# The MLP residual of a decoder trunk: added up in SBUF, or gathered per group and added in DRAM by accumulating DMAs

## The chip, the cores and the metric

One Trainium2 chip, one of its cores. The metric is the device time of one execution in microseconds (us), lower is better. Before the change three executions took 2427.35, 2429.12 and 2431.06 us; the median is 2429.12 us.

## The reference

A two-layer decoder trunk, sequence 1024, width 1024, all in float32. Layer 0 mixes with an mLSTM, layer 1 with differential attention that reads a K/V shared between layers. Both layers end in the same MLP, and that is all that the change touches:

```python
y = modulate(rms_norm(x, norm_mlp_g[layer]), sh2, sc2)
x = x + g2 * sq_relu_mlp(y, mlp_w_up[layer], mlp_w_down[layer])   # square(relu(y @ w_up)) @ w_down
```

`x` is 1024 x 1024, `w_up` 1024 x 4096, `w_down` 4096 x 1024; the gate `g2` is one number for each column of `x`. After layer 0, `x` goes on to the attention layer, after layer 1 to the final norm.

## The kernel before, in words

Everything is kept transposed: a tile has 128 of the 1024 features on its partitions and 512 tokens along its free axis. The residual `xt` (the tile `x` of the profile) is one SBUF tile of 128 x 2 halves of the tokens x 8 feature blocks (nb) x 512, 4 MB. Each matmul is done three times, as high x high, low x high and high x low part of a split of both operands (`mm3`, lines 183 to 185), so each weight that arrives as `wraw`, `e` or `m` is split by ScalarE (ACT, line 170, the high part: `wh`, `eh`, `lh`) and then VectorE (DVE, line 171, the rest: `wl`, `el`, `ll`).

The MLP's 4096 hidden features are cut into 8 groups of 4 blocks. For groups 1 to 7 of each layer a group runs as follows. **Up** (`group_up`): 8 products of 24 matmuls for 4 weight blocks f0 to f3 and two halves; ACT takes relu and square, and ACT and DVE make from the results the operands `bh`, `bl`, `th`, `tl`. **Down** (`down`): the output's 8 blocks are taken as 4 pairs, 0 to 3; each pair's product is a 2 x 2 block product of Strassen's kind in Winograd's form, with 7 products instead of 8, each of 6 matmuls (3 for each of k = 0, 1). The seven of a pair are numbered 1 to 7, and `PSEQ` lists the order (pair, product) of all 28, which interleaves the pairs. The results of products 1, 6, 7 and 4 pile up in one PSUM bank, and those of 5 and 3 in another; after each product the bank as it stands is added, times the gate, into one of the pair's four cells of `xt` (`add`, line 675): cell (half 0, first block) receives 1 and 2, (half 1, first) 6 and 3, (half 1, second) 7 and 5, (half 0, second) 4. All 28 additions are DVE instructions that read PSUM and read and write `xt`.

A pair's weights come in two loads of 256 KB, `e` and `m` (lines 652, 653). DVE builds from them four sums in chain (lines 654 to 657: `m`, `e`, `e`, `m`), ACT and DVE split both into `eh`, `el` (needed by products 1, 2, 5, 6) and `lh`, `ll` (3, 4, 7). Raw and split weights share one pool of nine 4 KB buffers (`wp`), so a load can only be issued once the tile nine allocations before it has been read for the last time. In layer 0 the same pool also carries the `adar` loads (line 149), background work of 512 KB each for the conditioning.

Group 8 goes another way: up as before, down as a plain product (`gemm`) whose consumer `residual` adds into `xt` with DVE (line 585) and starts the sum of squares for the next norm.

Nothing of the order is written out beyond this. A scheduler (`schedule_with_timeline_sim=True`) puts the instructions on the engines' queues by its own simulation, so the same source line can land in another place when something near it changes. All loads and stores before the change are issued on SP's queue, which takes them strictly in order.

Of the kernel before, what the change touches and what calls it, by code (L numbers as in the profile page):

```python
# [12 lines left out]
ALU = mybir.AluOpType  # L13
# [41 lines left out]
def tile_yoco(ctx: ExitStack, tc: tile.TileContext, x, c, pos, cst, vec, bg, lp, ada,  # L55
              w_in, w_v0, w_v, w_o, w_mo, w_kv, w_vb, w_q, w_do, w_up, w_dn, out):
    nc = tc.nc
    pe, act, dve, sp = nc.tensor, nc.scalar, nc.vector, nc.sync
# [6 lines left out]
    def gps():  # L65
        return pools["g"].tile([P, HT], F32, tag="g", name="gps")
# [28 lines left out]
    xdr = dr.tile([P, 2, NB, HT], F32, tag="xdr", name="xdr")  # L95
# [66 lines left out]
    def mcol(l, which, nb):  # L162
        return mod[:, l * 48 + which * 8 + nb:l * 48 + which * 8 + nb + 1]
# [18 lines left out]
    def mm3(ps, wh, wl, a, b, first, last, more=False):  # L182
        pe.matmul(ps, lhsT=wh, rhs=a, start=first, stop=False, skip_group_check=more)  # L183
        pe.matmul(ps, lhsT=wh, rhs=b, start=False, stop=False, skip_group_check=more)  # L184
        pe.matmul(ps, lhsT=wl, rhs=a, start=False, stop=last, skip_group_check=more)  # L185
# [132 lines left out]
    def load_x(xt, src):  # L318
        for half in range(2):
            for k in range(0, NB, 4):  # L320
                sp.dma_start(out=xt[:, half, k:k + 4], in_=src[:, half, k:k + 4])
# [8 lines left out]
    xt = xp.tile([P, 2, NB, HT], F32, tag="x", name="x")  # L330
# [93 lines left out]
    with ExitStack() as ph:  # L424
# [39 lines left out]
        with ExitStack() as ph1:  # L464
            trp = ph1.enter_context(tc.tile_pool(name="tr", bufs=1))
            rows = trp.tile([AH, 3, T], F32, tag="rows", name="rows")
            for j, src in enumerate((ic, lf)):
                for half in range(2):
                    ps = pm.tile([P, HT], F32, tag="mb", name="rps")
# [4 lines left out]
            ps = pm.tile([P, HT], F32, tag="mb", name="mps")  # L474
# [4 lines left out]
        ps = pm.tile([P, HT], F32, tag="mb", name="mps")  # L479
# [117 lines left out]
    def mlp(np_, l, xt, slot, nbg, ends, args, before=None, tail=None, closing=()):  # L597
# [3 lines left out]
        with ExitStack() as ph:  # L601
# [16 lines left out]
                dve.tensor_tensor(out=out, in0=a, in1=b, op=ALU.subtract)  # L618

            quads = {}  # L620

            def quad_out(f, half, ps):
                j, q = f // 2, quads.setdefault(f // 2, {})
                q[f % 2, half] = squared(ps)

                def keep(hs, ls, i, src):
                    split(hs[:, i, j], ls[:, i, j], src)

                if (0, 0) in q and (0, 1) in q and "t1" not in q:
                    q["t1"] = scratch("t1")  # L630
                    sub(q["t1"], q[0, 1], q[0, 0])
                    keep(th, tl, 0, q["t1"])
                if (0, 0) in q and (1, 0) in q and "v" not in q:
                    q["v"] = scratch("v")
                    sub(q["v"], q[1, 0], q[0, 0])
                    keep(bh, bl, 0, q[0, 0])
                    keep(bh, bl, 1, q[1, 0])
                if (1, 1) in q:
                    b22, t1, t3, v = q[1, 1], q["t1"], q[0, 1], q["v"]
                    sub(t1, b22, t1)  # L640
                    keep(th, tl, 1, t1)
                    sub(t3, b22, t3)
                    sub(v, v, t3)
                    keep(th, tl, 2, t3)
                    keep(bh, bl, 2, b22)
                    keep(th, tl, 3, v)
                    del quads[j]
# [20 lines left out]
                      7: (th, tl, 2)}  # L668

            def down(pairs, ready):  # L670
                banks = {}

                def add(ps, half, nb):
                    xs = xt[:, int(half), nb]
                    dve.scalar_tensor_tensor(xs, ps, mcol(l, 5, nb), xs, ALU.mult, ALU.add)  # L675

                for i, p in PSEQ:
                    if p == 1:
                        if i + 1 < 4:
                            pairs[i + 1] = pairs[i + 1]()  # L680
                        else:
                            ready()
                    c = {1: "X", 6: "X", 7: "X", 4: "X", 5: "Y", 3: "Y", 2: "Z"}[p]
                    fresh = (i, c) not in banks
                    if fresh:
                        banks[i, c] = gps()
                    ps = banks[i, c]
                    wh, wl, wi = pairs[i][p]
                    hh, hl, hi = moving[p]
                    for k in range(2):  # L690
                        mm3(ps, wh[:, k, wi], wl[:, k, wi], hh[:, hi, k], hl[:, hi, k], fresh and k == 0,
                            k == 1, not fresh)
                    add(ps, p in (6, 7, 5, 3), 2 * i + (p in (7, 4, 5)))

            def dn_src(gi, nb, pat, **kw):
                b = ((gi * NB) + nb) * P * P * FN
# [24 lines left out]
            for gi in range(FG - 1):  # L721
                srcs = [[dn_src(gi, 2 * i + j, "(p q r c) -> p q r c", q=2, r=2) for j in range(2)] for i in range(4)]
                for got in group_up(gi, w0, steady if gi else first, lambda: pair_load(srcs[0])):
                    if isinstance(got, dict):
                        pairs = [got] + [lambda i=i: pair_load(srcs[i]) for i in range(1, 4)]
                    else:
                        quad_out(*got)
                nxt = []
                down(pairs, lambda: nxt.append(wload(w_up[l, FN * (gi + 1)], [P, NB, P], nbg and nbg + 1)))
                w0 = nxt[0]  # L730

            hh = hp.tile([P, 2, FN, HT], F32R, tag="th", name="hh")
            hl = hp.tile([P, 2, FN, HT], F32R, tag="tl", name="hl")
            sums = hp.tile([P, 2, HT], F32, tag="bh", name="sums")
            acc[:] = [sums[:, 0], sums[:, 1]]
            srcs = [dn_src(FG - 1, nb, "(p k c) -> p k c", k=FN) for nb in range(NB)]
            gi = FG - 1
            for got in group_up(gi, w0, steady, lambda: None):
                if got is None:
                    continue  # L740
                f, half, ps = got
# [14 lines left out]
    def resident(ph, name):  # L756
        xp = ph.enter_context(tc.tile_pool(name="xp" + name, bufs=1))
        np_ = ph.enter_context(tc.tile_pool(name="np" + name, bufs=6))
        pools["g"] = ph.enter_context(tc.tile_pool(name="pg" + name, bufs=7, space=PSUM))
        pools["n"] = ph.enter_context(tc.tile_pool(name="pn" + name, bufs=1, space=PSUM))  # L760
        rings.append(np_)
        return xp.tile([P, 2, NB, HT], F32, tag="x", name="x"), np_
# [3 lines left out]
    xt, np_ = resident(l0, "1")  # L766
# [15 lines left out]
    def q_norm(half):  # L782
# [5 lines left out]
        return f  # L788

    mlp(np_, 0, xt, 1, 2, ((0,), (1,)), {(1,): dict(hooks={1: q_norm(0)})}, lambda: scale_cols(3, 48 + 8, V_NMIX + 8),  # L790
        q_norm(1), (accs, vps))
    assert not pend
# [88 lines left out]
    with ExitStack() as ph:  # L881
# [172 lines left out]
        for i in range(len(seq) + 2 + LAG):  # L1054
# [17 lines left out]
            while norms and norms[0][0] < i - LAG:  # L1072
                h, half = norms[0][1:3]
# [19 lines left out]
    with ExitStack() as ph:  # L1093
        xt, np_ = resident(ph, "2")
        load_x(xt, xdr)
        scale_cols(4, 48 + 32, V_NMLP + 8)
        gemm([w_do[n] for n in range(8)], NB, yhk, ylk, residual(np_, xt, lambda nb: mcol(1, 2, nb), True), 0,
             (1,), hooks={1: mlp_norm(np_, 1, xt, 4)})

        def scaled(part, rb):  # L1100
            half, c0, c1 = (part, 0, HT) if isinstance(part, int) else part
            for k in range(NB):
                xs = cut(xt, part, k)
                dve.scalar_tensor_tensor(xs, xs, vc[:, V_FIN + k:V_FIN + k + 1], rb, ALU.mult, ALU.mult)
                if k % 2:
                    sp.dma_start(out=out[:, half, k - 1:k + 1, c0:c1], in_=cut(xt, part, slice(k - 1, k + 1)))

        ends = (1, 0, CUT), (1, CUT, HT)
        rbs = []
        def finish():  # L1110
            with tc.issue_after(added[0].ins):
                rbs.append(rstd_of(np_, ends[1]))
                for part, rb in zip(ends, rbs):
                    scaled(part, rb)

        mlp(np_, 1, xt, 4, 0, ((0,), ends), {ends: dict(
            hooks={1: lambda: scaled(0, rstd_of(np_, 0))}, sizes=LSZ,
            after={(len(LSZ) - 1, ends[0]): lambda: rbs.append(rstd_of(np_, ends[0]))})}, tail=finish,
            closing=(accs,))
# [99 lines left out]
```

## Time and profile before

| what | value |
|---|---|
| three executions, median | 2429.12 us (2427.35 to 2431.06) |
| the profiled execution's own time | 2429.98 us |
| its span, first to last instruction | 2428.2 us |
| TensorE (PE) busy | 2367.1 us, 97% |
| VectorE (DVE) busy | 1559.4 us, 64% |
| ScalarE (ACT) busy | 989.2 us, 41% |
| GpSimd (POOL) busy | 0.2 us; it issues nothing |
| DMA | 266.81 MB, 110 GB/s over the span |
| the changed line's group, L675 | 392 instructions, 286.8 us, 746 ns each |

The MLP of layer 0 runs from about 480 to 1160 us of the span, that of layer 1 from about 1740 to 2428 us. Times in a timeline are microseconds from the start of the span; a row has its start, its length, the engine, the line, the operation, output<-inputs and, in brackets, how long the engine had been idle before and what released it. SPq is SP's queue of DMA issues; its length is the issue, not the transfer.

### The profile page before, as it was taken

The numbers are of one execution on the slowest core, as the hardware profiler recorded it, in microseconds if no ns is written. First come the engines' busy times: TensorE is split into PE (matmuls) and PEld (weight loads), VectorE is DVE, ScalarE is ACT, GpSimd is POOL, SyncE is SP. The second block draws the span as 40 slices with busy tenths as digits, with TensorE's granted clock in tenths as the row PEclk, the third lists the DMA queues.
The fourth block names the chain that finished last, engine by engine and source line by source line (L and its number), as shares of the span: only waits on it lengthen the run. The fifth ranks groups of instructions, "written<-read, shape, count | busy, mean of one in ns | idle before, by whom it ended". The sixth has DMA issues, their size and how long they took to land.

```text
span 2428.2 us, 30918 instructions
## 1 busy us (share of the span) xinstructions
PE 2367.1 (97%) x12018; PEld 1983.7 (82%) x12018; DVE 1559.4 (64%) x2576; ACT 989.2 (41%) x1898; POOL 0.2 (0%) x4
## 2 busy tenths in 40 slices
PE   7999999999999999999999999999999999999997
PEld 4899998788888888887788899987778888878886
DVE  7436544787877787767653367664775567566647
ACT  4325633444324323424332467763434323432423
POOL 0000000000000000000000000000000000000000
PEclk9999999999999999999999999999999999999999
DMA  7312242313322342234454654764111111111113
GB/s 306 120 64 77 79 148 78 122 51 119 135 95 79 130 139 75 90 113 143 153 178 154 176 162 148 217 196 160 65 57 35 61 61 44 39 61 57 35 53 122
DMA packets 117150, 266.81 MB, mean 110 GB/s; under 512 B 12426, under 2 KB 51850, under 8 KB 115212
## 3 DMA queue, kind: packets, MB, share of 16 engines
q1 hardware_dynamic: 117004, 264.84, 33.5%
q8 instruction: 94, 1.54, 0.3%
q14 instruction: 52, 0.43, 0.1%
HBM read 228.03 MB, written 36.77 MB: 109 GB/s over the span
## 4 chain that ended last, share of the span: by engine, by line
PE 90%; DVE 3%; DMA 3%; ACT 2%; issue 1%; SPq 1%; DVEq 0%; ACTq 0%
PE gps L183 24%; PE gps L185 24%; PE gps L184 24%; PE gps L255 3%; PE gps L256 3%; PE gps L257 3%; PE gps L971 2%; PE sc L930 1%; PE sc L931 1%; PE tps L957 1%; DMA kb<-kdr 1%; DVE adar L336 1%; PE hps L528 1%; DMA wraw<-in_w_do_dram 1%; PE hps L530 1%
## 5 line engine op out<-in xcount | busy, mean ns | idle before, releaser
L183 PE MATMUL gps<-yh,wh 128*128 128x512 f32 x1664 | 657.4, 399 | 7.9 <-ACT yh L301 5.0
L184 PE MATMUL gps<-yl,wh 128*128 128x512 f32 x1664 | 658.5, 396 | 0.7 <-DVE yl L302 0.7
L185 PE MATMUL gps<-yh,wl 128*128 128x512 f32 x1664 | 655.3, 396 | 0.7 <-DVE wl L171 0.7
L183 PEld LDWEIGHTS gps<-yh,wh 128*128 128x128 f32 x1664 | 313.6, 189 | 85.4 <-ACT yh L301 5.9
L185 PEld LDWEIGHTS gps<-yh,wl 128*128 128x128 f32 x1664 | 313.4, 188 | 78.7 <-DVE wl L171 1.1
L184 PEld LDWEIGHTS gps<-yl,wh 128*128 128x128 f32 x1664 | 313.5, 188 | 76.7 <-issue 1.2
L170 ACT CAST wh<-wraw 128x1024 fp32r<-128x1024 f32 (+2 forms) x176 | 170.6, 970 | 473.7 <-DMA wraw<-in_w_up_dram 208.9
L171 DVE TENSOR_TENSOR wl<-wraw,wh 128x1024 fp32r<-128x1024 f32 (+2 forms) x176 | 198.1, 1126 | 206.3 <-ACT wh L170 204.5
L675 DVE SCALAR_TENSOR_TENSOR x<-gps,mod,x 128x512 f32<-128x512 f32 x392 | 286.8, 746 | 59.7 <-PE gps L185 58.1
L255 PE MATMUL gps<-wh,yh 128*128 128x256 f32 (+1 forms) x768 | 224.9, 293 | 4.8 <-ACT sv L841 3.4
L256 PE MATMUL gps<-wl,yh 128*128 128x256 f32 (+1 forms) x768 | 220.6, 287 | 0.0
L257 PE MATMUL gps<-wh,yl 128*128 128x256 f32 (+1 forms) x768 | 219.9, 286 | 0.0
L170 ACT CAST eh<-e 128x1024 fp32r<-128x1024 f32 x56 | 58.8, 1049 | 240.9 <-DVE e L656 240.9
L150 DVE CUSTOM_DVE_ANT_0 adar<-adar,sil 128x1024 f32<-128x1024 f32 x96 | 117.0, 1223 | 59.8 <-DMA adar<-in_ada_dram 59.2
L255 PEld LDWEIGHTS gps<-wh,yh 128*128 128x128 f32 x768 | 146.7, 191 | 6.5 <-ACT sv L841 3.6
L256 PEld LDWEIGHTS gps<-wl,yh 128*128 128x128 f32 x768 | 146.9, 191 | 1.0
L257 PEld LDWEIGHTS gps<-wh,yl 128*128 128x128 f32 x768 | 146.6, 191 | 0.7
L613 ACT ACTIVATE b<-gps 128x512 f32<-128x512 f32 x112 | 66.9, 597 | 186.9 <-PE gps L185 181.9
L940 ACT ACTIVATE pf<-sc,mx 128x256 f32<-128x256 f32 (+7 forms) x128 | 95.1, 748 | 18.1 <-DVE mx L934 10.4
L171 DVE TENSOR_TENSOR el<-e,eh 128x1024 fp32r<-128x1024 f32 x56 | 68.4, 1222 | 46.2 <-PE gps L184 44.2
L183 PE MATMUL gps<-th,lh 128*128 128x512 f32 x224 | 88.5, 395 | 0.3 <-DVE x L675 0.3
L185 PE MATMUL gps<-th,ll 128*128 128x512 f32 x224 | 88.4, 395 | 0.0
(257 smaller groups left out, 3832.6 us busy)
## 6 DMA issues: line engine op xcount, KB each, us to landing
adar<-in_ada_dram SPq DMA_DIRECT2D x112, 512.0 KB, 4.3
wraw<-in_w_up_dram SPq DMA_DIRECT2D x64, 512.0 KB, 3.3
e<-in_w_dn_dram SPq DMA_DIRECT2D x56, 256.0 KB, 3.0
m<-in_w_dn_dram SPq DMA_DIRECT2D x56, 256.0 KB, 3.0
x<-in_x_dram SPq DMA_DIRECT2D x8, 1024.0 KB, 9.2
wraw<-in_w_mo_dram SPq DMA_DIRECT2D x16, 512.0 KB, 3.2
wraw<-in_w_dn_dram SPq DMA_DIRECT2D x32, 256.0 KB, 2.6
ka<-kdr SPq DMA_DIRECT2D x32, 256.0 KB, 6.8
```

Of the source, the lines that this page charges most:

```text
L150: dve.tensor_tensor_reduce(r, r, sil, 1.0, 0.0, ALU.mult, ALU.add, mod[:, n:n + 1])
L170: act.copy(out=ph, in_=src)
L171: dve.tensor_tensor(out=pl, in0=src, in1=f32(ph), op=ALU.subtract)
L183: pe.matmul(ps, lhsT=wh, rhs=a, start=first, stop=False, skip_group_check=more)
L184: pe.matmul(ps, lhsT=wh, rhs=b, start=False, stop=False, skip_group_check=more)
L185: pe.matmul(ps, lhsT=wl, rhs=a, start=False, stop=last, skip_group_check=more)
L255: pe.matmul(ps, lhsT=a, rhs=wh[:, k % 4], start=k == 0, stop=False)
L256: pe.matmul(ps, lhsT=a, rhs=wl[:, k % 4], start=False, stop=False)
L257: pe.matmul(ps, lhsT=b, rhs=wh[:, k % 4], start=False, stop=k == NB - 1)
L613: act.activation(dst, ps, AF.Relu)
L675: dve.scalar_tensor_tensor(xs, ps, mcol(l, 5, nb), xs, ALU.mult, ALU.add)
L940: act.activation(pf[f][:, 0:n * P], pp[f][:, 0:n * P], AF.Exp, bias=mx[:, f:f + 1], accum_out=ls[:, f, qb % 4:qb % 4 + 1])
```

## The change

At the start of each MLP the residual is copied from `xt` to the DRAM tile `xdr` (both halves in layer 0; in layer 1 half 1 only, since half 0 is there from the attention). From then on `xt` holds no residual but, for each pair, the group's own sum: the first result for a cell is written by ACT (`act.mul`, products 1, 5, 6, 4), a second is added by DVE as before (products 2, 7, 3). When the seventh result of a pair is in, GpSimd's queue issues one DMA of 1 MB that adds the pair's 2 x 2 cells onto `xdr` in DRAM. Before group 8 the whole of `xt` is loaded back from `xdr` in four loads of 1 MB.

```diff
             quads = {}
+            for half in range(l, 2):
+                sp.dma_start(out=xdr[:, half], in_=xt[:, half])
...
             def down(pairs, ready):
-                banks = {}
-
-                def add(ps, half, nb):
+                banks, seen = {}, {}
+
+                def add(ps, half, nb, again):
                     xs = xt[:, int(half), nb]
-                    dve.scalar_tensor_tensor(xs, ps, mcol(l, 5, nb), xs, ALU.mult, ALU.add)
+                    if again:
+                        dve.scalar_tensor_tensor(xs, ps, mcol(l, 5, nb), xs, ALU.mult, ALU.add)
+                    else:
+                        act.mul(out=xs, in_=ps, mul=mcol(l, 5, nb))
...
-                    add(ps, p in (6, 7, 5, 3), 2 * i + (p in (7, 4, 5)))
+                    add(ps, p in (6, 7, 5, 3), 2 * i + (p in (7, 4, 5)), p in (2, 3, 7))
+                    seen[i] = seen.get(i, 0) + 1
+                    if seen[i] == 7:
+                        nc.gpsimd.dma_start(out=xdr[:, :, 2 * i:2 * i + 2], in_=xt[:, :, 2 * i:2 * i + 2],
+                                            accum_op=ALU.add)
...
             hl = hp.tile([P, 2, FN, HT], F32R, tag="tl", name="hl")
+            load_x(xt, xdr)
             sums = hp.tile([P, 2, HT], F32, tag="bh", name="sums")
```

The scheduler answers with another order. Three places of it follow, each before and then after; line numbers shift by up to 10 (675 becomes 678, 654 to 657 become 656 to 659).

PE, down half of a steady group of layer 1, where pair 2 begins. `eh`, `el` are here pair 2's weights, `lh`, `ll` those of the pairs before it:

```order
L183 MATMUL gps<-th,lh 128x512
L184 MATMUL gps<-tl,lh 128x512
L185 MATMUL gps<-th,ll 128x512
L183 MATMUL gps<-th,lh 128x512
L184 MATMUL gps<-tl,lh 128x512
L185 MATMUL gps<-th,ll 128x512
L183 MATMUL gps<-bh,eh 128x512
L184 MATMUL gps<-bl,eh 128x512
L183 MATMUL gps<-th,eh 128x512
L184 MATMUL gps<-tl,eh 128x512
L183 MATMUL gps<-bh,eh 128x512
L184 MATMUL gps<-bl,eh 128x512
```

```order
L183 MATMUL gps<-bh,eh 128x512
L184 MATMUL gps<-bl,eh 128x512
L183 MATMUL gps<-th,eh 128x512
L184 MATMUL gps<-tl,eh 128x512
L183 MATMUL gps<-bh,eh 128x512
L184 MATMUL gps<-bl,eh 128x512
L183 MATMUL gps<-th,lh 128x512
L184 MATMUL gps<-tl,lh 128x512
L185 MATMUL gps<-th,ll 128x512
L183 MATMUL gps<-th,lh 128x512
L184 MATMUL gps<-tl,lh 128x512
L185 MATMUL gps<-th,ll 128x512
```

Both pieces start at the same place of PE's queue: pair 2's first six matmuls now stand ahead of the six of product 4 of pair 0, where they stood behind them.

DVE, the same place: the four sums of pair 2's weights, its two splits, and the additions into `x` that stand between them:

```order
L654 TENSOR_TENSOR m<-e,m 128x2x128
L655 TENSOR_TENSOR e<-m 128x2x128
L675 SCALAR_TENSOR_TENSOR x<-gps,mod,x 128x512
L656 TENSOR_TENSOR e<-e 128x2x128
L675 SCALAR_TENSOR_TENSOR x<-gps,mod,x 128x512
L657 TENSOR_TENSOR m<-e 128x2x128
L171 TENSOR_TENSOR el<-e,eh 128x1024
L675 SCALAR_TENSOR_TENSOR x<-gps,mod,x 128x512
L171 TENSOR_TENSOR ll<-m,lh 128x768
```

```order
L656 TENSOR_TENSOR m<-e,m 128x2x128
L657 TENSOR_TENSOR e<-m 128x2x128
L678 SCALAR_TENSOR_TENSOR x<-gps,mod,x 128x512
L658 TENSOR_TENSOR e<-e 128x2x128
L659 TENSOR_TENSOR m<-e 128x2x128
L678 SCALAR_TENSOR_TENSOR x<-gps,mod,x 128x512
L171 TENSOR_TENSOR el<-e,eh 128x1024
L678 SCALAR_TENSOR_TENSOR x<-gps,mod,x 128x512
L171 TENSOR_TENSOR ll<-m,lh 128x768
```

The addition ahead of the third sum, on which `eh` waits, stays; the next one moves from ahead of the fourth sum to behind it.

SP, end of group 7 of layer 0: the last weights of the down half, then group 8's f0 to f3 (`in_w_up`) among the background loads:

```order
L653 DMA m<-in_w_dn_dram 128x2x256
L175 DMA wraw<-in_w_up_dram 128x1024
L149 DMA adar<-in_ada_dram 128x1024 x3
L175 DMA wraw<-in_w_up_dram 128x1024
L149 DMA adar<-in_ada_dram 128x1024 x2
L175 DMA wraw<-in_w_up_dram 128x1024
L149 DMA adar<-in_ada_dram 128x1024
L175 DMA wraw<-in_w_up_dram 128x1024
```

```order
L655 DMA m<-in_w_dn_dram 128x2x256
L175 DMA wraw<-in_w_up_dram 128x1024
L321 DMA x<-xdr 128x2048 x2
L149 DMA adar<-in_ada_dram 128x1024 x3
L175 DMA wraw<-in_w_up_dram 128x1024
L149 DMA adar<-in_ada_dram 128x1024 x2
L175 DMA wraw<-in_w_up_dram 128x1024
L149 DMA adar<-in_ada_dram 128x1024
L175 DMA wraw<-in_w_up_dram 128x1024
L321 DMA x<-xdr 128x2048 x2
```

Two of the four loads of the residual, those of blocks 0 to 3, now stand between f0 and f1; the other two follow f3. The first two wait for the accumulating DMAs of pairs 0 and 1, the last two for those of pairs 2 and 3. In layer 1 the first two stand in the same place, without the background loads, and the last two come after the first weights of the down half of group 8.

## The prediction

> **What bounds the kernel now.** I read the page first, then the busy time in windows laid over the MLPs, then who waits for the changed line, then one pair's load in the timeline.
>
> ```profile
> PE 2367.1 (97%) x12018; PEld 1983.7 (82%) x12018; DVE 1559.4 (64%) x2576; ACT 989.2 (41%) x1898; POOL 0.2 (0%) x4
> ...
> 480.00:700.00 220.00, 220.00 (x949) 177.80 (x948) 174.00 (x275) 86.46 (x128) 0.00 (x0) 1.00 0.28 93
> ...
> 1755.00:1955.00 200.00, 199.75 (x858) 160.76 (x857) 130.20 (x200) 76.41 (x113) 0.00 (x0) 1.00 0.15 48
> 1955.00:2155.00 200.00, 199.93 (x861) 161.05 (x860) 132.00 (x197) 65.52 (x91) 0.00 (x0) 1.00 0.17 54
> 2155.00:2355.00 200.00, 200.00 (x862) 161.61 (x861) 119.71 (x177) 69.14 (x101) 0.00 (x0) 1.00 0.15 49
> ```
>
> The columns of a window are its length, then PE, weight loads, DVE, ACT and POOL (busy us, count), the granted clock, DMA share, GB/s. PE is busy for 599.68 of the 600 us of layer 1's groups and for all of a window of layer 0, at a granted clock of 1.00; 858 matmuls in 200 us are one each 0.233 us. PE sets the end here, and what it does is not changed: a gain can only come out of the holes that it has in these groups, and there is next to nothing to take.
>
> ```profile
> L675 DVE SCALAR_TENSOR_TENSOR x<-gps,mod,x x392: 737/746/754, 513.4 to 2329.9; 128x512 f32<-128x512 f32 x196
> ...
> who waited for it (us, times):
>   PEld gps L183: 2.6, 10
>   PE gps L183: 0.3, 1
> ```
>
> The 392 additions take 746 ns each, but in the whole run PE waited 2.9 us for them. That is the ceiling of the gain on this path.
>
> The margin on the other side is thin. Pair 2's weights in a group of layer 1, from the release of a buffer to the first matmul, then pair 3's:
>
> ```profile
> 1956.72 0.40 PE L184 MATMUL gps<-tl,eh 128*128 128x512 f32 x1
> 1957.14 0.54 SPq L653 DMA_DIRECT2D m<-in_w_dn_dram  x1
> 1960.08 0.43 DVE L654 TENSOR_TENSOR m<-e,m 128x256 f32<-128x256 f32 x1 [0.51 <-DMA m<-in_w_dn_dram]
> 1960.76 0.75 DVE L675 SCALAR_TENSOR_TENSOR x<-gps,mod,x 128x512 f32<-128x512 f32 x1
> 1961.92 1.05 ACT L170 CAST eh<-e 128x1024 fp32r<-128x1024 f32 x1 [8.27 <-DVE e L656]
> 1963.01 1.23 DVE L171 TENSOR_TENSOR el<-e,eh 128x1024 fp32r<-128x1024 f32 x1 [0.17 <-ACT eh L170]
> 1964.12 0.39 PE L183 MATMUL gps<-bh,eh 128*128 128x512 f32 x1
> ...
> 1964.26 0.55 SPq L652 DMA_DIRECT2D e<-in_w_dn_dram  x1
> 1964.91 0.55 SPq L653 DMA_DIRECT2D m<-in_w_dn_dram  x1
> 1968.13 0.43 DVE L654 TENSOR_TENSOR m<-e,m 128x256 f32<-128x256 f32 x1 [0.76 <-DMA m<-in_w_dn_dram]
> 1969.96 1.05 ACT L170 CAST eh<-e 128x1024 fp32r<-128x1024 f32 x1 [6.21 <-DVE e L656]
> ...
> 1972.36 0.40 PE L183 MATMUL gps<-bh,eh 128*128 128x512 f32 x1
> ```
>
> PE's last use of `eh` of pair 0 (1956.72) frees the buffer for `m`; the load lands at about 1960.0, `eh` is ready at 1961.92 + 1.05 = 1962.97, and PE takes it at 1964.12: 1.15 us to spare. Pair 3 has 1972.36 - 1971.01 = 1.35 us. So the kernel is bound by PE with two transfers a group, 28 in all, that arrive about a microsecond early. Layer 0 is alike:
>
> ```profile
> 945.99 1.05 ACT L170 CAST eh<-e 128x1024 fp32r<-128x1024 f32 x1 [8.17 <-DVE e L656]
> ...
> 948.13 0.39 PE L183 MATMUL gps<-bh,eh 128*128 128x512 f32 x1
> ```
>
> There pair 2 has 948.13 - 947.04 = 1.09 us.
>
> **The change part by part.** *The additions.* Of 28 in a group, 16 go from DVE to ACT; DVE loses 16 x 0.746 = 11.9 us a group, ACT gains 16 times what it takes for the same shape out of PSUM:
>
> ```profile
> L613 ACT ACTIVATE b<-gps 128x512 f32<-128x512 f32 x112 | 66.9, 597 | 186.9 <-PE gps L185 181.9
> ```
>
> 16 x 0.6 = 9.6 us. ACT was busy for 65 to 76 us of each 200, so 9.6 us in the roughly 84 us of a group (360 matmuls x 0.233) stay hidden behind PE. I credit 0.8 us for holes that close, between 0 and the 2.9 us above.
>
> *Pair 2's weights.* The order shows its first six matmuls moved ahead of six others, 6 x 0.233 = 1.4 us earlier, while the chain that makes `eh` keeps its steps: the same release, the same load, and still one addition (1960.76) before the third sum. `eh` would be wanted at 1964.12 - 1.40 = 1962.72 and is there at 1962.97; PE loads weights one matmul ahead, 0.23 us more. So about 0.5 us of stall, and since PE has nothing else in its order, it adds to the end: 14 groups x 0.5 = 7 us. Lower bound 0 (the addition in the chain is early and costs nothing: 0.66 us back), upper bound 1.1 us a group (an ACT addition of 0.6 us holds up the cast): 0 to 15. I take 7, being the rows as they stand.
>
> *Pair 3's weights.* In the built program its `e` waits for product 4 of pair 0, which is now six matmuls later; its `m` waits for pair 2's `ll`. Product 4's last read of `lh` stands 32 matmuls ahead of pair 3's first, at 1972.36 - 7.46 = 1964.90; with the 0.42 us that 1956.72 to 1957.14 shows, `e` is issued at 1965.3 and `m` 0.65 us later at 1966.0, 1.1 us later than before. Of 1.35 us 0.25 us remain, which the weight load uses up. The accumulating DMA of pair 0 is issued at that same moment, since product 4 is also the last that it needs: it runs beside these 512 KB. What the DMA engines move at most:
>
> ```profile
> 1680.00:1690.00 10.00, 6.68 (x25) 4.54 (x24) 3.64 (x8) 2.15 (x7) 0.00 (x0) 0.83 0.89 354
> ```
>
> At 354 GB/s 512 KB need 1.45 us, at half of it 2.9: at worst 1.45 us late, at best nothing. I take 0.5, as the accumulation starts about 0.6 us (ACT) after the loads are issued: 14 x 0.5 = 7 us, bounds 0 to 20. f0 of the next group is safe: its first matmul moves back by 12 in the order.
>
> *The accumulating DMA itself* is in no row. It reads 1 MB of SBUF and 1 MB of DRAM and writes 1 MB. The nearest rows:
>
> ```profile
> xdr<-x SPq DMA_DIRECT2D x2, 2048.0 KB, 8.2
> ...
> x<-xdr SPq DMA_DIRECT2D x4, 1024.0 KB, 11.3
> ```
>
> Lower bound: half of the plain store of 2 MB, 4.1 us. Upper bound: read, read and write one behind the other, 12.3 us. I take 8.2 us, that of a plain 2 MB, since two operands have to be read. Four of them are 33 us in a group of 84.
>
> The Trainium skill ("Collectives: The Full Stack", section "The bandwidth ceiling: the fold count and why AG ≠ RS ≠ AR") says that a DMA that adds runs at half the rate of one that copies, because it reads two sources, not because of the addition. No run here shows it yet; by it the estimate is the value that I take, and a copy's rate would lower the sum by the next term.
>
> *The reload ahead of group 8.* This is the wait that the change adds: SP stops at the first `x<-xdr` until pair 1's accumulation has landed, and behind it stand f1 and, in layer 0, three background loads.
>
> ```profile
> adar<-in_ada_dram SPq DMA_DIRECT2D x112, 512.0 KB, 4.3
> wraw<-in_w_up_dram SPq DMA_DIRECT2D x64, 512.0 KB, 3.3
> ...
> 1049.28 0.33 SPq L175 DMA_DIRECT2D wraw<-in_w_up_dram  x1
> ...
> 1054.49 1.05 ACT L170 CAST wh<-wraw 128x1024 fp32r<-128x1024 f32 x1 [11.43 <-DVE mod L150]
> ```
>
> Before, f1 was issued at 1049.28 and split from 1054.49 on. In the new order 116 matmuls, 27.0 us, lie between pair 1's last and f1's first. Clock from the former's end: pair 0's accumulation is issued at -3.2 (18 matmuls earlier, plus 1 us for matmul end and ACT); f0's 0.5 MB pass beside it (1.5 us at 354 GB/s); two accumulations as 2 MB each of traffic, 5.9 us apiece, are through at about 11 and landed at 12.5. Then SP sends 2 MB of residual, 1.5 MB of background and 0.5 MB of f1, 11.3 us, while pair 2's accumulation takes its 5.9 us of the same engines: 29.7, landed 31.2, split 32.7. That is 5.7 us late in layer 0; without the background loads in layer 1 (7.1 + 5.9, plus landing and split) 28.5, 1.5 us late. Starting costs on GpSimd's queue have no row; with 1.5 us each side I take 10 us for both layers. Bounds: 0 with accumulations of 4.1 us, 35 (22 and 13) with 12.3.
>
> *The stores at the start* hide, by these rows:
>
> ```profile
> 382.53 61.33 SPq L175 DMA_DIRECT2D wraw<-in_w_mo_dram  x11
> ...
> 469.44 0.33 SPq L175 DMA_DIRECT2D wraw<-in_w_up_dram  x1
> ```
>
> The first store of layer 0 stands on SP among these loads, issued one each 5.6 us with two of them ahead of PE, so 11 us cover its 8.2. The second stands ahead of f3, issued at 469.44 and used shortly before the first addition at 513.4; that of layer 1 stands behind f3. Cost 0, and up to 8 if that cover were gone.
>
> **Sum**: 7 + 7 + 10 - 0.8 = +23 us against the profiled execution's own 2429.98 us (span 2428.2 and 1.8 around it): 2453. That execution is 0.9 us above the median of the three, so I forecast **2452 us**; own range 2436 to 2472.
>
> **The rivals.**
> - *Not slower.* At the rate of a plain copy (4.1 us) f1 arrives in time, and the freed DVE makes pairs 2 and 3 as early as their new places ask: the four sums and splits of a pair then no longer queue behind 16 additions. For it: DVE is busy 130 of 200 us, in the down half nearly always. Against: the order keeps the addition in the chain of `eh`. Time: 2429 + 0 to 4, say 2431. It decides if an accumulation lasts under about 5 us.
> - *Faster.* The PE waits for additions go, 2.9 us, and nothing else is lost: 2426; more than that no row offers.
> - *The accumulations choke the loads.* At 12 us or more, four fill 49 us and more of a group's 84, and each load of pairs 2 and 3 meets one: a load's 2.9 us doubled, of which 0.5 is in the sum, 14 x 2 x 2.4 = 67; with 35 instead of 10 for the reloads 2452 + 67 + 25 = 2544. For it: all share the same 16 engines. Against: the DMA share is only 0.15 to 0.28 now.
>
> The Trainium skill ("DMA: Bandwidth & Descriptors", section "Queues, rings and completion order") says that each DMA engine takes turns between queues by the packet. If accumulated packets are slow, a load then waits for one of them at each of its own packets: that is how the last rival would come about. No run here shows it yet.
>
> **How the numbers follow.** Forecast 0.60; not slower 0.20; choked 0.16; faster 0.04. A measurement of this kernel tells about 0.2%, 4.9 us, from no change. The faster case reaches that bound only at its edge, so faster 0.04, same 0.20, slower 0.76. The range takes in the forecast, most of "not slower" and the beginning of the third: 2431 to 2486.
>
> **What would show it.** After: the group of ACT additions with 224 instructions near 0.6 us and 168 left on DVE; GpSimd's DMAs in the table of issues with a landing near 8 us; holes of about 0.5 us in PE ahead of `eh` of pairs 2 and 3, released by ACT; a hole of 2 to 8 us in each layer ahead of f1 of group 8, with SP waiting before `x<-xdr`. I am wrong if PE stays as full as before (then the two spare microseconds were larger than read), or if the holes are before other weights (f0, `lh`), or if landings beyond 12 us stand in the table.

## The result, and the profile after

The kernel after the change takes 2454.07 us (median of 4 executions, 2452.08 to 2458.38), the kernel before, beside it on the same chip, 2428.23 us (4, 2425.32 to 2431.06): slower by 1.1%, ratio 1.0109 with a 95% interval of 1.0096 to 1.0123. The profiled execution took 2453.39 us, 23.4 us more than the profiled one of before; its span is 2451.6 us.

The page after, with the totals, the group of ACT's additions and the row of GpSimd's DMA queue (packets, MB, share of the time of all 16 DMA engines):

```profile
PE 2370.2 (97%) x12018; PEld 1981.5 (81%) x12018; DVE 1411.7 (58%) x2352; ACT 1129.2 (46%) x2122; POOL 61.2 (2%) x60
...
q0 software_dynamic: 15232, 58.72, 12.9%
...
L680 ACT ACTIVATE x<-gps,mod 128x512 f32<-128x512 f32 x224 | 152.7, 686 | 180.8 <-PE gps L185 180.7
```

The work moved as planned: DVE has 148 us less, ACT 140 us more, and PE does what it did (3 us more busy time, from slower matmuls, of which below). The end got nothing from it, since PE sets it. The same windows as before the change:

```profile
480.00:700.00 220.00, 217.69 (x929) 173.51 (x929) 147.96 (x236) 109.92 (x167) 8.84 (x8) 1.00 0.48 132
1755.00:1955.00 200.00, 199.37 (x856) 160.38 (x856) 111.84 (x172) 100.79 (x151) 8.71 (x8) 1.00 0.38 89
...
2155.00:2355.00 200.00, 193.32 (x820) 154.94 (x819) 94.96 (x139) 88.02 (x128) 10.87 (x10) 0.98 0.48 117
```

PE, full to within 0.3 us in all of these before, now lacks 2.3, 0.6 and 6.7 us. DVE fell from 119.71 to 94.96 us in the last window, where PE lost most. Three places carry the loss.

**Pair 2's weights.** A steady group of layer 1, from the timeline:

```profile
1971.99 0.43 DVE L656 TENSOR_TENSOR m<-e,m 128x256 f32<-128x256 f32 x1 [1.53 <-DMA m<-in_w_dn_dram]
...
1972.67 0.75 DVE L678 SCALAR_TENSOR_TENSOR x<-gps,mod,x 128x512 f32<-128x512 f32 x1
...
1973.33 0.42 DVE L658 TENSOR_TENSOR e<-e 128x256 f32<-128x256 f32 x1
...
1973.78 1.05 ACT L170 CAST eh<-e 128x1024 fp32r<-128x1024 f32 x1 [2.71 <-DVE e L658]
...
1974.16 0.40 PE L185 MATMUL gps<-th,ll 128*128 128x512 f32 x1
1974.88 0.50 PE L183 MATMUL gps<-bh,eh 128*128 128x512 f32 x1 [0.32 <-ACT eh L170]
1975.21 0.40 PE L184 MATMUL gps<-bl,eh 128*128 128x512 f32 x1
```

ACT had been idle for 2.71 us when it could cast `eh`: it is not ACT's new work that is late, but the chain load, sums, one addition, sum, cast, which has kept its length, while PE comes to `eh` six matmuls earlier. From 1974.16 to 1975.21 two steps of PE take 1.05 us instead of 0.47: 0.58 us lost, of which the row's idle time shows 0.32 (matmuls overlap, and the first one behind a wait is slower). Who waits for the tile `eh` in the whole run (us, times):

```profile
  PE gps L183: 4.4, 13
```

One of the 13, of 0.68 us, is in the first group of layer 0; the others and a shorter one are pair 2's in the 13 groups that follow, 0.38 to 0.68 us each from start to start, 7.4 us together.

**The reload ahead of group 8.** Layer 1, from the timeline:

```profile
2319.91 0.40 PE L185 MATMUL gps<-th,ll 128*128 128x512 f32 x1
...
2321.33 1.09 POOL L701 DMA_DIRECT2D xdr<-x  x1 [3.09 <-DVE x L678]
...
2333.43 1.60 SPq L321 DMA_DIRECT2D x<-xdr  x2
...
2335.07 1.58 SPq L175 DMA_DIRECT2D wraw<-in_w_up_dram  x2
...
2343.10 0.39 PE L183 MATMUL gps<-yh,wh 128*128 128x512 f32 x1
...
2346.39 1.04 ACT L170 CAST wh<-wraw 128x1024 fp32r<-128x1024 f32 x1 [14.29 <-DMA wraw<-in_w_up_dram]
...
2347.47 1.23 DVE L171 TENSOR_TENSOR wl<-wraw,wh 128x1024 fp32r<-128x1024 f32 x1 [12.92 <-ACT wh L170]
2348.61 0.75 DVE L678 SCALAR_TENSOR_TENSOR x<-gps,mod,x 128x512 f32<-128x512 f32 x1
...
2349.41 0.80 PE L183 MATMUL gps<-th,lh 128*128 128x512 f32 x1 [5.92 <-DVE x L678]
2350.01 0.63 PE L184 MATMUL gps<-tl,lh 128*128 128x512 f32 x1
2350.43 0.63 PE L185 MATMUL gps<-th,ll 128*128 128x512 f32 x1
```

The first row is the last matmul of pair 1. Read upwards from PE. It does not wait for f1; it stands before a product of pair 3, whose PSUM bank has not been added out, because that addition (2348.61) is behind `wl` of f1 in DVE's queue (2347.47). DVE waited 12.92 us for `wh`, ACT 14.29 us for f1's data, and SP could not ask for f1 before the two reloads, which had to wait for the accumulation issued at 2321.33 to land. Layer 0 has the same with a background load in f1's place, 4.68 us of idle time. After the hole the matmuls start 0.42 to 0.43 us apart instead of 0.23, at a granted clock of 0.56 in the window 2349.40 to 2354.00.

**The first group of layer 0** lost 1.8 us of busy time in the window 480 to 530, which is quoted at the fifth experiment, in four holes; with 0.26 us beside the idle time of each, as above, some 2.8 us.

### The profile page after: what moved, and what is told of

Its sections match the earlier page's. It is cut to its first block, busy times and chain, and to the rows that moved or that the text cites. A ratio compares the mean times of both kernels' runs of the same rounds, so it can differ in the third digit from the quotient of the medians.

```text
span 2451.6 us, 31152 instructions
## 1 busy us (share of the span) xinstructions
PE 2370.2 (97%) x12018; PEld 1981.5 (81%) x12018; DVE 1411.7 (58%) x2352; ACT 1129.2 (46%) x2122; POOL 61.2 (2%) x60
## 3 DMA queue, kind: packets, MB, share of 16 engines
q0 software_dynamic: 15232, 58.72, 12.9%
## 4 chain that ended last, share of the span: by engine, by line
PE 83%; DMA 8%; DVE 5%; ACT 2%; issue 1%; SPq 1%; DVEq 0%; ACTq 0%
PE gps L183 22%; PE gps L185 21%; PE gps L184 21%; PE gps L255 3%; PE gps L256 3%; PE gps L257 3%; PE gps L981 2%; DMA m<-in_w_dn_dram 2%; DMA wraw<-in_w_up_dram 1%; PE sc L940 1%; PE sc L941 1%; PE tps L967 1%; DMA adar<-in_ada_dram 1%; DMA xdr<-x 1%; DVE adar L336 1%
## 5 line engine op out<-in xcount | busy, mean ns | idle before, releaser
L183 PE MATMUL gps<-yh,wh 128*128 128x512 f32 x1664 | 657.2, 399 | 8.6 <-ACT yh L301 5.2
L184 PE MATMUL gps<-yl,wh 128*128 128x512 f32 x1664 | 658.4, 396 | 0.8 <-DVE yl L302 0.8
L183 PEld LDWEIGHTS gps<-yh,wh 128*128 128x128 f32 x1664 | 313.3, 188 | 87.2 <-ACT yh L301 6.5
L184 PEld LDWEIGHTS gps<-yl,wh 128*128 128x128 f32 x1664 | 313.7, 189 | 76.8 <-issue 1.2
L680 ACT ACTIVATE x<-gps,mod 128x512 f32<-128x512 f32 x224 | 152.7, 686 | 180.8 <-PE gps L185 180.7
L678 DVE SCALAR_TENSOR_TENSOR x<-gps,mod,x 128x512 f32<-128x512 f32 x168 | 125.5, 748 | 110.4 <-PE gps L185 59.2
L701 POOL DMA_DIRECT2D xdr<-x x56 | 61.0, 1090 | 2293.3 <-ACT x L680 2135.2
L183 PE MATMUL gps<-th,lh 128*128 128x512 f32 x224 | 89.4, 399 | 10.6 <-DVE x L678 10.6
## 6 DMA issues: line engine op xcount, KB each, us to landing
xdr<-x POOLq DMA_DIRECT2D x56, 1024.0 KB, 10.5
```

Of the source, the lines that this page charges most:

```text
L680: act.mul(out=xs, in_=ps, mul=mcol(l, 5, nb))
```

## The experiments

The kernel before ran beside them: medians 2427.59 us (experiments 1 to 4), 2426.52 (5 to 8) and 2426.34 us (9 and 10). A ratio takes in every execution of both kernels, so it is not exactly the quotient of the two medians.

### 1. The reload from another queue

```diff
-            load_x(xt, xdr)
+            for half in range(2):
+                for k in range(0, NB, 4):
+                    nc.gpsimd.dma_start(out=xt[:, half, k:k + 4], in_=xdr[:, half, k:k + 4])
```

> The four reloads of the residual ahead of group 8 are issued from GpSimd's queue instead of SP's; PE's order in groups 1 to 7 stays that of the change. Theory A (waits in queues: SP stands before the reload, f1 and the background loads stand behind it, and DVE's queue behind their data): the holes of 5.08 us (layer 0) and 6.31 us (layer 1) and the matmuls at half pace behind them, 7.4 + 8.2 = 15.6 us together, go; 2454 - 15.6 = 2438 us. Pair 2's holes, 6 us, stay. Rival B (the traffic does it: 2 MB of reload and the accumulations share the DMA engines with f1): f1 is late whoever issues the reload; 2448 to 2454 us, with holes of 3 us and more left ahead of group 8.

Measured: 2438.28 us, ratio 1.0035 (1.0022 to 1.0049). The windows around the two holes, first after the change:

```profile
1060.00:1080.00 20.00, 15.32 (x57) 11.96 (x56) 9.42 (x15) 4.18 (x7) 1.09 (x1) 0.83 0.93 322
2335.00:2355.00 20.00, 14.07 (x53) 10.95 (x52) 4.30 (x5) 5.02 (x7) 1.09 (x1) 0.83 0.64 219
```

and with the reload moved:

```profile
1060.00:1080.00 20.00, 20.00 (x87) 16.12 (x86) 9.29 (x14) 5.76 (x9) 1.34 (x2) 1.00 1.04 320
2335.00:2355.00 20.00, 20.00 (x87) 16.12 (x86) 9.05 (x12) 7.07 (x12) 2.23 (x3) 1.00 0.89 227
```

PE does 30 and 34 matmuls more in them, 64 x 0.233 = 14.9 us, and the median falls by 15.8. The same bytes pass in the same stretch (a DMA share of 1.04 and 0.89, not less than before): it was the place in SP's queue, not the traffic. B falls for this term.

### 2 and 3. PE's order at pair 2 against ScalarE's share

Which of the first additions ACT takes decides what order the scheduler gives PE: with product 6 on ACT alone PE keeps the moved order, with products 1, 5 and 4 on ACT and 6 on DVE it returns to the old one at pairs 2 and 3. The two edits are drawn as one here.

```diff
-                    else:
+                    elif p in on_act:        # experiment 2: (6,); experiment 3: (1, 5, 4)
                         act.mul(out=xs, in_=ps, mul=mcol(l, 5, nb))
+                    else:
+                        dve.tensor_scalar(out=xs, in0=ps, scalar1=mcol(l, 5, nb), scalar2=None, op0=ALU.mult)
```

> Of the 16 first additions of a group ScalarE keeps only those of product 6 (4); the others go to VectorE as plain multiplications. PE's order at pair 2 is still the moved one (its first six matmuls ahead of product 4 of pair 0). Theory A (the moved order makes pair 2's holes, since eh is wanted 1.4 us earlier than it is made): 14 holes of 0.3 us or more ahead of eh stay, and are no smaller since VectorE, which makes the sums for eh, has more to do; 2454 to 2462 us. Rival C (ScalarE's additions hold up the cast of eh): with 4 instead of 16 of them the holes go; about 2448 us.

> The counterpart: ScalarE keeps the first additions of products 1, 5 and 4 (12 of 16), product 6 goes to VectorE. PE's order at pair 2 is then that of the kernel before; accumulating DMAs and reload stay. Theory A: the 14 holes ahead of pair 2's eh go, 6 us less: 2448 us; the holes ahead of group 8 stay. Rival C (ScalarE's additions): with 12 of 16 left, holes of 0.3 us or more stay; 2452 to 2454 us.

Measured: 2454.35 us, ratio 1.0117 (1.0089 to 1.0144), and 2440.53 us, ratio 1.0061 (1.0041 to 1.0080). Who waits for `eh`, with the moved order:

```profile
  PE gps L183: 3.6, 13
```

and with the old order:

```profile
  PE gps L183: 0.7, 1
```

(the one left is in the first group of layer 0). With four additions on ACT the 13 waits are there, with twelve they are gone: the order makes them, and C falls. The second kernel came out 8 us better than expected because its order on SP moved too, in layer 1:

```profile
2314.26 6.28 SPq L175 DMA_DIRECT2D wraw<-in_w_up_dram  x2
2323.13 0.80 SPq L321 DMA_DIRECT2D x<-xdr  x2
```

f0 and f1 are issued there, and then the reload; with f1 ahead of it layer 1 has no hole at all, which is the first experiment's result in another way.

### 4. Without the accumulating DMAs

```diff
-                    seen[i] = seen.get(i, 0) + 1
-                    if seen[i] == 7:
-                        nc.gpsimd.dma_start(out=xdr[:, :, 2 * i:2 * i + 2], in_=xt[:, :, 2 * i:2 * i + 2],
-                                            accum_op=ALU.add)
```

> The accumulating DMAs are left out (the sums of groups 1 to 7 then do not reach the residual); additions, stores at the start, reload and PE's order at pair 2 stay. Theory A: pair 2's holes, 6 us, and those of group 1 of layer 0, 2.5 us, stay, since they owe nothing to this traffic; the reload waits for no accumulation, is issued some 10 us earlier, and the holes ahead of group 8 go: 2438 us. Rival B (the accumulations' traffic makes the loads late): pair 2's holes go too; 2431 us.

Measured: 2437.11 us, ratio 1.0042 (1.0028 to 1.0057), A's number. Who waits for `eh`:

```profile
  PE gps L183: 3.5, 13
```

Pair 2's waits owe nothing to the new traffic. And beside experiment 1, at 2438.28 us with all of the traffic, no cost of the accumulations themselves can be told in this order (the medians are 1.2 us apart, the ratios, 1.0035 and 1.0042, lie the other way); what they cost in the change, they cost through the reload that waits for them.

### 5. The stores at the start from another queue

```diff
-                sp.dma_start(out=xdr[:, half], in_=xt[:, half])
+                nc.gpsimd.dma_start(out=xdr[:, half], in_=xt[:, half])
```

> The stores of the residual at the start of each MLP are issued from GpSimd's queue instead of SP's; all else as in the change. Theory A (in layer 0 the second store waits on SP for half 1 and pushes the background loads and pair 0's weights behind it 6.5 us back, from 486.40 to 492.92): the holes of group 1 of layer 0, about 2.5 us, go; 2451.5 us. Rival B (the stores' 4 MB of traffic, or ScalarE's and VectorE's new order in the first group, make the holes): nothing goes; 2454 us.

Measured: 2453.17 us, ratio 1.0114 (1.0091 to 1.0137), not to be told from the change. The window of the first group, after the change and then here:

```profile
480.00:530.00 50.00, 48.17 (x202) 37.23 (x202) 41.48 (x68) 31.16 (x51) 0.00 (x0) 1.00 0.17 53
```

```profile
480.00:530.00 50.00, 49.51 (x212) 39.23 (x211) 41.53 (x68) 31.44 (x51) 0.00 (x0) 1.00 0.17 53
```

1.3 of the 1.8 us come back. The trace is on A's side, the time is too coarse to say so.

### 6. Copies in place of additions

The slices are written as `...` in this edit and the next.

```diff
-                        nc.gpsimd.dma_start(out=xdr[...], in_=xt[...], accum_op=ALU.add)
+                        nc.gpsimd.dma_start(out=xdr[...], in_=xt[...])
```

> The DMAs of the pairs copy instead of adding (a pair's sum replaces the residual in DRAM; the addition is left out); orders as in the change. Theory D (a DMA that adds takes twice as long as one that copies, as my 8.2 us over 4.1 us supposed): the DMA from GpSimd's queue lands in 5 to 6 us instead of 10.5, the reload is issued 4 to 5 us earlier in each layer and the holes ahead of group 8 shrink from 7.4 + 8.2 us to about 4 together: 2442 us. Rival E (the time is that of 1 MB from this queue, whether it adds or not): landing 10 us, holes as they are, 2454 us.

Measured: 2437.66 us, ratio 1.0049 (1.0029 to 1.0069). From the page, GpSimd's queue and the landing of its DMAs:

```profile
q0 software_dynamic: 15232, 58.72, 6.0%
...
xdr<-x POOLq DMA_DIRECT2D x56, 1024.0 KB, 6.2
```

and layer 1's window of the reload:

```profile
2335.00:2355.00 20.00, 20.00 (x87) 16.13 (x86) 8.00 (x11) 6.34 (x11) 0.00 (x0) 1.00 0.49 181
```

The same packets and bytes take 6.0% of the DMA engines' time instead of 12.9%, a ratio of 2.15, and land in 6.2 us instead of 10.5 (quoted below). So D holds: a DMA that adds occupies the engines about twice as long. The Trainium skill ("Collectives: The Full Stack", section "The bandwidth ceiling: the fold count and why AG ≠ RS ≠ AR") has the factor of two, for the reduce step of a collective, which reads two sources. This trace agrees in the engines' time (2.15 times); the landing is 1.7 times as long, and that the second read is the reason no run here shows. With the reload freed 4 us earlier the holes ahead of group 8 did not shrink to 4 us but went, while pair 2's stay (`eh` is waited for 15 times, 4.5 us). The profiled execution is the fastest of the five (2432.38 us, the slowest 2443.16), and its stretch between the MLPs is some 6 us shorter than after the change, with PE's order the same; so only the windows are read here.

### 7. Twice the accumulations

```diff
                         nc.gpsimd.dma_start(out=xdr[...], in_=xt[...], accum_op=ALU.add)
+                        nc.gpsimd.dma_start(out=xd2[...], in_=xt[...], accum_op=ALU.add)
```

(`xd2` is a second DRAM tile, filled at the start; reloads as in experiment 1.)

> The reloads on GpSimd's queue as in the first experiment, and each pair's sum is added a second time onto another DRAM tile that nobody reads: twice the accumulating traffic. Theory A (the traffic costs nothing while no load is queued behind it): 2438 us, as with the reload moved alone, at most 2 us more. Rival B (accumulating traffic slows the loads of pairs 2 and 3): those loads land later, holes ahead of the eh of pair 3 appear and those of pair 2 grow: 2445 us and more.

Measured: 2490.30 us, ratio 1.0269 (1.0249 to 1.0289). The table of DMA issues, with the landing in us at the end of a row:

```profile
adar<-in_ada_dram SPq DMA_DIRECT2D x112, 512.0 KB, 11.8
xdr<-x POOLq DMA_DIRECT2D x56, 1024.0 KB, 18.9
...
wraw<-in_w_up_dram SPq DMA_DIRECT2D x64, 512.0 KB, 10.5
e<-in_w_dn_dram SPq DMA_DIRECT2D x56, 256.0 KB, 3.1
```

and the two MLPs as windows:

```profile
480.00:1180.00 700.00, 659.20 (x2742) 523.09 (x2741) 411.37 (x643) 298.10 (x446) 63.13 (x60) 0.97 0.71 185
1800.00:2455.00 655.00, 653.16 (x2823) 526.69 (x2822) 342.56 (x512) 304.15 (x454) 63.18 (x60) 1.00 0.63 147
```

Who waits for `wh`, the high part of the up weights (`mm3` stands a line further down in this kernel, so L184 is its first matmul; before the change the same wait was 0.6 us, 2 times):

```profile
  PE gps L184: 31.1, 11
```

Both theories miss: B has the time (2445 us and more), but not the place. The traffic does choke loads, against A, but not those of pairs 2 and 3, against B: `e` lands in 3.1 us as ever (the median; pair 3's is issued just before the accumulations of its group begin, at 905.90 against 907.12 in one group). Late are the up weights and the background loads behind them. PE is idle for 40.8 of the 700 us of layer 0, and with the matmuls at half the clock behind the holes it does 2742 where a full window holds 3004 (700 / 0.233): some 61 us lost. In layer 1, where the same doubled traffic runs beside half the loads, it is idle for 1.8 us and loses no more than that.

Not all of the 61 us is the accumulations' doing. From 480 to 500 us PE does 55 matmuls against 87 in experiment 1, about 7 us lost, and the first accumulation is issued only at 539.64. What is new ahead of that is the filling of `xd2`, which layer 1 does not have: its second half is issued at 468.34, a background load at 468.47, and VectorE waits 12.10 us for that load's data, 7.56 in experiment 1, before it gets to the norm. So the traffic was one doubling away from the rival that I had given 0.16, by another door.

### 8 to 10. All three mended, and what is left

Reloads as in 1, stores as in 5, first additions as in 3; then the same without the accumulating DMAs, and the same with all first additions on DVE.

> Together: reloads and stores on GpSimd's queue, and product 6's first additions on VectorE, which gives PE its old order at pair 2. Theory A (queues and order are all of the loss, 15.6 + 6 + 2.5 us of 26): 2429 to 2431 us, no difference that can be told from the kernel before. Rival B (56 accumulating DMAs and 16 MB of stores and reloads have a cost of their own): 2435 us or more.

> The kernel of all three mendings (2436.87 us, 0.5% above the kernel before) with the accumulating DMAs left out (the sums of groups 1 to 7 then do not reach the residual); PE's order at pairs 2 and 3, the stores and the reloads on GpSimd's queue stay. Theory F (what is left is the accumulations' traffic: it makes loads of w_up and adar later, 4.8 and 5.4 us to landing against 3.3 and 4.3 before): 2427 to 2430 us, and w_up lands in 3.3 to 3.6 us. Rival G (what is left is the sharing with ScalarE, the stores and the reloads: additions that stand in VectorE's queue behind late work): 2435 us or more, with the same small holes.

> The kernel of all three mendings with every first addition on VectorE as a plain multiplication: nothing is shared with ScalarE, the accumulating DMAs, stores and reloads on GpSimd's queue stay. Theory F (traffic): as with the three mendings, 2435 to 2439 us, w_up still lands in about 4.8 us. Rival G (ScalarE's share and the order that it brings): the small holes ahead of th and lh go, 2430 us.

Measured: 2436.87 us (ratio 1.0051, 1.0033 to 1.0068), 2429.16 us (1.0011, 1.0002 to 1.0020) and 2440.63 us (1.0055, 1.0043 to 1.0068). A fell at the eighth: three causes worth 25 us by the traces (14.9, 7.4, 2.8), and their mending together gains 17. The ninth tells why, in part. In the eighth kernel, the landing of the up weights and layer 1's window:

```profile
wraw<-in_w_up_dram SPq DMA_DIRECT2D x64, 512.0 KB, 4.8
```

```profile
1750.00:2390.00 640.00, 638.58 (x2738) 513.50 (x2738) 350.60 (x525) 280.52 (x416) 32.38 (x32) 1.00 0.43 103
```

and the same two views of the ninth, without the accumulations:

```profile
wraw<-in_w_up_dram SPq DMA_DIRECT2D x64, 512.0 KB, 3.3
```

```profile
1750.00:2390.00 640.00, 640.00 (x2756) 516.92 (x2755) 352.93 (x528) 282.07 (x417) 2.16 (x4) 1.00 0.18 57
```

F holds for the times of the eighth and the ninth: of the 10 us left, 8 go with the traffic, and the up weights land as fast as before the change. Taking ACT out altogether gains nothing; the tenth kernel is even above F's 2439 us, with up weights that land in 5.8 us, not 4.8.

By which way the traffic costs 8 us is shown in part only. Without it PE does 18 matmuls more in layer 1's window (2756 against 2738, 4.2 us), but none more in layer 0 (2948 against 2950 from 480 to 1180 us), and the two profiled executions are 4.7 us apart, not 8. A likely way is f0 of the next group: in the old order of PE it is wanted 12 matmuls earlier than in the change's, and the accumulations of pairs 0 and 1 run while it loads. PE's L183 waits for `wh` 6.7 us, 12 times, in the tenth kernel, but only 1.8 us, 4 times, in the eighth; it is 0.5 us, once, in the ninth and 0.9 us, 3 times, after the change. That the order which costs 7.4 us at pair 2 also hides the traffic would explain why the ninth experiment finds a price of the accumulations where the fourth finds none; it is argued, not shown. None of these kernels beats the kernel before.

## Why the prediction was right, and where it was not

The forecast was 2452 us (range 2431 to 2486), the time is 2454. Term by term, against 23.4 us in the profiled executions (the terms measure 25; the rest is in stretches that the change does not touch, and smaller than what two executions of one kernel differ by):

- *The additions* (gain of 0.8, ACT 0.6 us each): ACT takes 686 ns, not 600, since a multiplication by a number for each partition is slower here than the relu that I took as the nearest row (595 ns in this trace). Hidden behind PE as supposed; what the gain came to was not measured apart.
- *Pair 2's weights*, 7: measured 7.4, at the place and by the chain that the order showed. Experiments 2, 3 and 4 leave nothing else.
- *Pair 3's weights*, 7: measured 0. The step that failed is the price in "I take 0.5, as the accumulation starts about 0.6 us (ACT) after the loads are issued", with the two sharing the engines from then on. The start came as said: GpSimd takes up the accumulation 0.59 us after `m` is issued (1978.35 to 1978.94). But the loads are through as fast as before:

```profile
1977.72 0.54 SPq L654 DMA_DIRECT2D e<-in_w_dn_dram  x1
...
1978.35 0.56 SPq L655 DMA_DIRECT2D m<-in_w_dn_dram  x1
...
1978.94 1.09 POOL L701 DMA_DIRECT2D xdr<-x  x1 [53.70 <-ACT x L680]
...
1981.55 0.43 DVE L656 TENSOR_TENSOR m<-e,m 128x256 f32<-128x256 f32 x1 [3.94 <-DMA m<-in_w_dn_dram]
...
1983.34 1.05 ACT L170 CAST eh<-e 128x1024 fp32r<-128x1024 f32 x1 [0.50 <-DVE e L658]
...
1984.75 0.39 PE L183 MATMUL gps<-bh,eh 128*128 128x512 f32 x1
```

From `m`'s issue to the first sum it is 3.20 us, before the change 3.22 (1964.91 to 1968.13). The rest of the step holds: `e` is issued 7.03 us ahead of pair 3's first matmul (1977.72 to 1984.75), where it was 8.10 (1964.26 to 1972.36), and `eh` is there at 1983.34 + 1.05 = 1984.39, 0.36 us to spare where 0.25 had been worked out. Why the accumulation does not slow loads issued just ahead of it is open.
- *The reload ahead of group 8*, 10: measured 14.9, more than its value and well inside its bounds. The chain up to f1 was read nearly right, in layer 1: the reload was issued 13.1 us after pair 1's last matmul (2319.91 + 0.40 to 2333.43) where I had 12.5, although an accumulation lands in 10.5 us, not 8.2, and f1 was split (2347.47 + 1.23) 28.4 us after it where I had 28.5. Mis-sized is what f1's lateness costs PE, above all in layer 1 ("28.5, 1.5 us late"): measured 34 matmuls, 7.9 us. I let PE run on to f1's first matmul. It stops earlier, before a product of pair 3, since DVE's queue has f1's `wl` ahead of the addition that frees the PSUM bank. And a hole of this length is followed by some ten matmuls at half the clock, about 2 us in each layer, for which the sum had no term. The Trainium skill ("TensorE: Matmul & The Clock Gate", "Part 1: The HAM clock gate") says that PE falls to half its clock after at least one idle window of about 3.4 us. The rows agree on the half clock (0.43 us apart after a hole of 5.92 us, 0.23 before it). They do not bear out 3.4 us as the least idle time that it takes: in the tenth experiment matmuls at a granted clock of 0.54 (1816.80 to 1820.50) stand behind a hole of 1.81 us (not behind every such hole: after the change there are none behind one of 1.56 us at 1698.58):

```profile
1816.81 0.67 PE L183 MATMUL gps<-yh,wh 128*128 128x512 f32 x1 [1.81 <-ACT wh L170]
1817.28 0.63 PE L184 MATMUL gps<-yl,wh 128*128 128x512 f32 x1
```

- *The stores at the start*, 0 with "up to 8 if that cover were gone": most of the 2.8 us of the first group (1.3 of its 1.8 us of idle time came back in experiment 5). The second store of layer 0 waits on SP and pushes what stands behind it.

So the sum came out within 2 us by luck: the 7 us that did not come were made up for by 5 at the reload and some 2 at the stores that I had too little. The mechanism of two of the four terms, the order at pair 2 and SP's queue at the reload, was right and is shown by the runs. One of the signs of being wrong did appear: the two longest holes stand before an `lh` product, not before f1's own matmuls, since the wait for f1 (in layer 0 for a background load) reaches PE through DVE's queue.

Of the rivals, "not slower" needed accumulations below about 5 us; a plain copy takes 6.2, and with it the reload's holes are indeed gone (experiment 6), but pair 2's stay. "Choked loads" was wrong at this traffic, and right at twice as much for the up weights, in layer 0.

The table of DMA issues after the change:

```profile
xdr<-x POOLq DMA_DIRECT2D x56, 1024.0 KB, 10.5
wraw<-in_w_up_dram SPq DMA_DIRECT2D x64, 512.0 KB, 6.0
```

Here too it is the up weights that land later (3.3 us before the change), not the weights of pairs 2 and 3.

## What to carry to other kernels

A load that has to wait for a slow transfer belongs on a queue on which nothing urgent stands behind it: moving four loads of each layer from SP's queue to GpSimd's was worth 15 us here, and no byte was saved by it. Work taken off an engine that was not the bound bought nothing here, while the new order that came with it was charged where a transfer had a microsecond to spare (at pair 2; pair 3 kept 0.36 us); so look for the tightest margins in the trace of before and at what the new order does to each. And price a late load by the first queue that it blocks, not by its own consumer, with the half clock after a hole of several microseconds added.

## What was not expected of the hardware

- The accumulating DMA of 1 MB from SBUF to DRAM lands in 10.5 us (median of 56), the plain one from the same queue in 6.2; engine time 12.9% against 6.0% for the same packets. Two accumulations at a time land in 18.9 and 25.4 us.
- Each costs GpSimd 1.09 us to issue (a plain copy of the same bytes 0.68, in experiment 6), three times the 0.33 us of a 512 KB load on SP.
- Causes do not add: mending three that the traces put at 15, 7 and 3 us gained 17. The 8 us between go with the accumulations' traffic (experiment 9); that the moved order had covered it is argued.
- With the traffic doubled PE is idle for 40.8 us in layer 0, some 61 us lost with the half clock behind the holes, and for 1.8 us in layer 1. That it is the background loads that tip it is argued from their landing, 11.8 us, and was not tried by itself; about 7 us of it came before the first accumulation, beside the filling of the second tile.
